# Places of activations in a line of 128 bytes, a block inverse in halves, and masks kept once

## The chip, the core and the metric

The kernel runs on one core of a Trainium2 chip. The core has a matmul engine (PE, whose weight loads are listed apart as PEld), three elementwise engines (DVE, ACT, POOL) and queues that start transfers (SP, ACT, POOL). A tile lies in the on-chip memory as 128 partitions with a line of bytes in each; matmuls write to PSUM, a second memory. The metric is device time in microseconds (us) of one execution; lower is better.

## What is computed

A small network on one sequence of 256 positions of width 1024: one block of four linear-attention mixers, cross-attention to a memory of 256 rows and a convolutional feed-forward layer; then two blocks of attention (three kinds of heads) and feed-forward. Cut to what the change touches, the second mixer solves a triangular system for each head and each chunk, here of 128 positions:

```python
kk    = where(strict, k @ k.T * ratio, 0)           # below the diagonal
a_mat = eye(c) + beta[:, None] * kk
u_v   = triangular_solve(a_mat, beta[:, None] * v, lower=True, unit_diagonal=True)
w_k   = triangular_solve(a_mat, (beta * gamma)[:, None] * k, lower=True, unit_diagonal=True)
```

Everything else that the change touches is products of float32 matrices: activations (256 positions) times weights.

## The kernel before, in words

Every large product is made from halves of the numbers: an activation or a weight `a` is kept as an upper part `hi` (float32r) and a rest `lo = a - hi`, and a product is three matmuls, hi by hi, lo by hi, hi by lo (`mm_f`, L429, L430, L431). In `mm_f` the weights are the stationary operand (128 columns), the activations the moving one (256 columns). `mm_t` (L440 to L442) has them the other way round. Weights arrive in chunks of 512 KB on SP's queue; ACT makes `whi` (L410) and DVE `wlo` (L411).

The activations' tiles are `xh` and `xl` (input of a stage, eight blocks of 256 columns), `oh`/`ol`, `xoh`/`xol`, `aoh`/`aol` (input of an output product), `gh`/`gl` (the feed-forward layer's inner width, 22 blocks) and `mh`/`ml` (the memory). One block is 1024 bytes in a partition, so all blocks of a tile begin at the same place in a line of 128 bytes; which place that is follows from what is allocated ahead of it. All weight blocks of 128 columns begin at place 0. `GPAD` (L50) is a tile of some columns ahead of `gh`, and moves it.

Stages follow one another: the mixers (`block1_mix`, to some 245 us), cross-attention (to 323), feed-forward f0 (`psU` is its upward product, `psD` its downward one, to 510), attention 0 (to 648), feed-forward l0f (to 832), attention 1, feed-forward l1f.

The triangular solve stands in `delta` (L852). It works on eight matrices of 128x128 (two chunks t, four heads h) in `An`, and builds the inverse by doubling the block size: at level k, blocks of b = 2^k are joined. `TT` is the inverse transposed, `Tm` the inverse. A level multiplies `An` with the left columns of `Tm` (`psy`, L980), masks (`Y`, DVE, L982), multiplies with `TT` (`psu`, L994) and adds to `Tm` (DVE, L995); then `Tm` is transposed on PE (`psw`, L1002) and copied to `TT` (ACT, L1003). There are six levels; the sixth adds to `TT` alone (L990). Each `yield` hands over to the next of three generators: `weave` (L778) runs `delta`, `hgrn` and `turns` in turn, and a scheduler orders the instructions of each engine from that.

The masks `triu` and `strict` lie in the tile `cst1`, and are copied by DVE to `levr` (L912, L913), whose first 896 columns come by a transfer from POOL's queue (L750).

Of the kernel before, what the change touches and what calls it, by code (L numbers as in the profile page):

```python
# [8 lines left out]
F32 = mybir.dt.float32  # L9
F32R = mybir.dt.float32r  # L10
# [6 lines left out]
P = 128  # L17
# [32 lines left out]
GPAD = {"f0": 8, "l0f": 16, "l1f": 72}  # L50
# [145 lines left out]
def const_arrays():  # L196
# [16 lines left out]
    c1["triu"] = (i[:, None] <= i[None, :])  # L213
    c1["strict"] = (i[:, None] > i[None, :])
# [20 lines left out]
    c1["mk"] = np.concatenate(mk[1:], 1)  # L235
    c1["decay"] = dec.reshape(P, -1)
    c1["lev"] = np.concatenate(lev, 1)
# [128 lines left out]
class Net:  # L366
# [27 lines left out]


# [143 lines left out]
    def xsplit(self, x, g, acts=None):  # L539
        xh, xl = acts or (self.act.tile([P, KD, T], F32R, tag="xh", name="xh"), self.act.tile([P, KD, T], F32R, tag="xl", name="xl"))  # L540
# [80 lines left out]
    def ffn(self, tag, g, fc, nt):  # L621
        nc = self.nc
        x = self.x
        xh, xl = self.xsplit(x, g)
        acc, = self.sumsq(x)
        with self.pool("ffn" + tag) as big, self.pool("fz" + tag, 3) as zp:
            big.tile([P, GPAD[tag]], F32, name="gpad")
            gh = big.tile([P, NFF, T], F32R, name="gh")
            gl = big.tile([P, NFF, T], F32R, name="gl")
# [72 lines left out]
    def block1_mix(self, es):  # L702
# [5 lines left out]
        n1 = _C1O["triu"][0]  # L708
# [6 lines left out]
        xh, xl = self.xsplit(x, self.par("mix"))  # L715
# [136 lines left out]
    def delta(self, s, sm, gates):  # L852
# [57 lines left out]
        tri, strict = self.c1("triu"), self.c1("strict")  # L910
# [46 lines left out]

        TM = b8.tile([P, 2, 2, 4, P], F32, tag="b8", name="TM")
        TT, Tm = TM[:, 0], TM[:, 1]
        idb = self.ident.unsqueeze(1).to_broadcast([P, 4, P])  # L960
        mi = lambda a: a.bitcast(I32)
        for t in range(2):
            nc.gpsimd.tensor_copy(TT[:, t], idb)
            odd = lambda a: a.rearrange("p h (n d) -> p h n d", d=2)[:, :, :, 1]
            nc.vector.copy_predicated(odd(TT[:, t]), mi(self.c1("mlev")[:, 0:64]).unsqueeze(1).to_broadcast([P, 4, 64]), odd(An[:, t]))
            pt = self.pb(512, "pstt")
            for h in range(4):
                self.tr(pt[:, h * P:(h + 1) * P], TT[:, t, h, :])
            nc.scalar.copy(fl(Tm[:, t]), pt)
        for k in range(1, 7):  # L970

            b = 1 << k
            mk = self.c1("mk")[:, (k - 1) * 64:k * 64].unsqueeze(1).to_broadcast([P, 4, 64])
            left = lambda a: a.rearrange("p h (n c d) -> p h n c d", c=2, d=b)[:, :, :, 0, :]
            yield
            Ys = []
            for t in range(2):
                py = self.pb(T, "psy")
                for h in range(4):
                    self.mm(py[:, h * 64:(h + 1) * 64].rearrange("p (n d) -> p n d", d=b), An[:, t, h, :], left(Tm[:, t])[:, h])  # L980
                Y = m.tile([P, 4, 64], F32, tag="Yl", name="Y", bufs=2)
                nc.vector.tensor_mul(Y, py.rearrange("p (h c) -> p h c", h=4), mk)  # L982
                Ys.append(Y)
            for t in range(2):
                Y = Ys[t]
                if k == 6:
                    pu = self.pb(512, "psu2")
                    for h in range(4):
                        self.mm(pu[0:64, h * P:(h + 1) * P], Y[:, h, :], TT[:, t, h, :])
                    nc.vector.tensor_add(fl(TT[0:64, t]), fl(TT[0:64, t]), pu[0:64])  # L990
                    continue
                pu = self.pb(T, "psu2")
                for h in range(4):
                    self.mm(pu[:, h * 64:(h + 1) * 64], TT[:, t, h, :], Y[:, h, :])  # L994
                nc.vector.tensor_add(left(Tm[:, t]), left(Tm[:, t]), pu.rearrange("p (h n d) -> p h n d", h=4, d=b))  # L995
            if k == 6:
                continue
            yield
            for t in range(2):
                pw = self.pb(512, "psw2")  # L1000
                for h in range(4):
                    self.tr(pw[:, h * P:(h + 1) * P], Tm[:, t, h, :])  # L1002
                nc.scalar.copy(fl(TT[:, t]), pw)  # L1003
# [276 lines left out]
    def keys_norm(self, mem):  # L1280
        nc = self.nc
        nc.sync.dma_start(mem, self.ap["memT"])
        self.mh = self.memp.tile([P, KD, T], F32R, name="mh")
        self.ml = self.memp.tile([P, KD, T], F32R, name="ml")
# [21 lines left out]
    def xattn(self, es):  # L1306
# [5 lines left out]
        xh, xl = self.xsplit(self.x, self.par("xat"))  # L1312
# [13 lines left out]
        oh = m.tile([P, KD, T], F32R, name="xoh")  # L1326
        ol = m.tile([P, KD, T], F32R, name="xol")
# [56 lines left out]
    def block2(self):  # L1384
# [5 lines left out]
        for l in range(2):  # L1390
            with ExitStack() as es:
                xh, xl = self.xsplit(x, self.par("ga1") if l else gg)
                self.attn(es, l, xh, xl)
# [6 lines left out]
        y = self.act.tile([P, KD, T], F32, tag="xh", name="y")  # L1400
# [23 lines left out]
    def attn(self, es, l, xh, xl):  # L1424
# [40 lines left out]
        self.mm_f(kk[0:96], a + "kk", range(KD), xh, xl)  # L1465
        lh = m.tile([P, 3, T], F32R, name="lath")
# [54 lines left out]
        oh = m.tile([P, KD, T], F32R, name="aoh")  # L1521
        ol = m.tile([P, KD, T], F32R, name="aol")
# [163 lines left out]
```

## Time and profile before

| | us |
|---|---|
| median of 3 runs | 1165.92 (1165.40 to 1167.05) |
| the profiled execution | 1163.74 |
| its span, first to last instruction | 1162.0 |
| PE busy | 1135.8 (98%) |
| DVE busy | 937.0 (81%) |
| ACT busy | 668.2 (58%) |

A matmul's record ends later than the next one's begins, so "busy" says that PE has work, not that it runs at its best. What a matmul costs in a row of them is the distance from start to start: the length of a stretch plus one duration, divided by the count of records that touch the stretch.

### The profile page before, as it was taken

To read this page: it belongs to the slowest core of one execution; us is meant where nothing else is said; L and a number is where in the kernel's file an instruction comes from. 1 tells how busy PE (TensorE), PEld (TensorE's weight loads), DVE (VectorE), ACT (ScalarE), POOL (GpSimd) and SP (SyncE) were. 2 spreads that over 40 slices of the span, in tenths; PEclk is the share of its full clock that TensorE was granted. 3 is DMA by queue.
4 is the path that set the end of the run, shared out by engine and by line. 5 is a ranking of instruction groups with operands and counts; after the bars stand their busy time and mean duration, and the time that the engine had idled before them with its cause. 6 is when DMAs were issued, how large, how long until landed. Compare 5 with 4: busy or idle time off the path is not lost.

```text
span 1162.0 us, 23197 instructions
## 1 busy us (share of the span) xinstructions
PE 1135.8 (98%) x9148; PEld 1093.9 (94%) x9148; DVE 937.0 (81%) x1887; ACT 668.2 (58%) x1178; POOL 109.9 (9%) x137
## 2 busy tenths in 40 slices
PE   7999999999999999999999999999999999999996
PEld 7899888989999999998989999999998999999996
DVE  7887869587589997559898899986588978999854
ACT  6652545565476666554555676665445557766642
POOL 5501201010010000222000200001120002000000
PEclk9899999999999999999999999999999999999998
DMA  6522242556446656554423565565553235555652
GB/s 246 171 73 79 69 143 76 171 176 220 133 153 199 199 187 195 183 179 134 137 94 110 181 185 196 183 190 194 185 162 125 92 128 182 183 193 187 187 194 85
DMA packets 51948, 184.68 MB, mean 159 GB/s; under 512 B 5888, under 2 KB 6784, under 8 KB 51584
## 3 DMA queue, kind: packets, MB, share of 16 engines
q1 hardware_dynamic: 51408, 182.23, 49.0%
q8 instruction: 71, 1.16, 0.4%
q10 hardware_dynamic: 288, 0.52, 0.1%
q0 software_dynamic: 144, 0.46, 0.1%
q14 instruction: 37, 0.30, 0.1%
HBM read 182.14 MB, written 1.05 MB: 158 GB/s over the span
## 4 chain that ended last, share of the span: by engine, by line
PE 89%; DVE 7%; ACT 2%; issue 1%; DMA 0%; SPq 0%; POOL 0%; DVEq 0%; ACTq 0%
PE psU L431 10%; PE psU L430 10%; PE psU L429 10%; PE psD L430 5%; PE psD L431 5%; PE psD L429 5%; PE psp L429 3%; PE po L451 3%; PE psp L430 3%; PE psp L431 3%; PE psW L429 3%; PE psW L431 3%; PE psW L430 2%; PE pst L442 2%; PE pst L440 2%; PE pst L441 2%
## 5 line engine op out<-in xcount | busy, mean ns | idle before, releaser
L410 ACT ACTIVATE whi<-raw 128x1024 fp32r<-128x1024 f32 (+5 forms) x411 | 362.9, 898 | 304.6 <-PE psU L430 53.7
L411 DVE TENSOR_TENSOR wlo<-raw,whi 128x1024 fp32r<-128x1024 f32 (+5 forms) x411 | 424.2, 1044 | 136.4 <-ACT whi L410 134.2
L429 PE MATMUL psU<-xh,whi 128*128 128x256 f32 x1056 | 295.4, 280 | 0.0
L431 PE MATMUL psU<-xh,wlo 128*128 128x256 f32 x1056 | 294.9, 279 | 0.2 <-DVE wlo L411 0.2
L430 PE MATMUL psU<-xl,whi 128*128 128x256 f32 x1056 | 294.8, 279 | 0.0
L431 PEld LDWEIGHTS psU<-xh,wlo 128*128 128x128 f32 x1056 | 198.5, 188 | 0.4 <-DVE wlo L411 0.4
L429 PEld LDWEIGHTS psU<-xh,whi 128*128 128x128 f32 x1056 | 198.5, 188 | 0.1
L430 PEld LDWEIGHTS psU<-xl,whi 128*128 128x128 f32 x1056 | 198.5, 188 | 0.1
L429 PE MATMUL psD<-gh,whi 128*128 128x256 f32 x528 | 146.8, 278 | 0.0
L430 PE MATMUL psD<-gl,whi 128*128 128x256 f32 x528 | 146.8, 278 | 0.0
L431 PE MATMUL psD<-gh,wlo 128*128 128x256 f32 x528 | 146.8, 278 | 0.0
L534 POOL TENSOR_TENSOR ssa<-ssa,ssq 128x256 f32<-128x256 f32 x61 | 56.5, 931 | 711.6 <-ACT ssq L532 440.7
L666 DVE SCALAR_TENSOR_TENSOR y<-zb,prm,y 128x256 f32<-128x256 f32 x264 | 113.9, 477 | 0.0
L430 PEld LDWEIGHTS psD<-gl,whi 128*128 128x128 f32 x528 | 99.2, 188 | 0.0
L431 PEld LDWEIGHTS psD<-gh,wlo 128*128 128x128 f32 x528 | 99.2, 188 | 0.0
L429 PEld LDWEIGHTS psD<-gh,whi 128*128 128x128 f32 x528 | 99.2, 188 | 0.0
L429 PE MATMUL psp<-xh,whi 128*128 128x256 f32 (+1 forms) x288 | 83.8, 291 | 0.0
L430 PE MATMUL psp<-xl,whi 128*128 128x256 f32 (+1 forms) x288 | 82.6, 287 | 0.0
L431 PE MATMUL psp<-xh,wlo 128*128 128x256 f32 (+1 forms) x288 | 82.4, 286 | 0.0
L657 ACT ACTIVATE y<-zb,prm 128x256 f32<-128x256 f32 x132 | 67.2, 558 | 6.6 <-DVE zb L653 6.6
L440 PE MATMUL pst<-whi,xh 128*128 128x256 f32 (+3 forms) x176 | 56.9, 324 | 0.0
L429 PEld LDWEIGHTS psp<-xh,whi 128*128 128x128 f32 (+1 forms) x288 | 54.2, 188 | 2.4 <-issue 2.3
(456 smaller groups left out, 2337.6 us busy)
## 6 DMA issues: line engine op xcount, KB each, us to landing
raw<-in_wst_dram SPq DMA_DIRECT2D x319, 512.0 KB, 3.5
raw<-in_wst_dram SPq DMA_DIRECT2D x5, 448.0 KB, 3.3
cst<-in_c_dram SPq DMA_DIRECT2D x1, 1664.0 KB, 7.4
raw<-in_wst_dram SPq DMA_DIRECT2D x3, 396.0 KB, 3.1
mem<-in_memT_dram SPq DMA_DIRECT2D x1, 1024.0 KB, 5.0
raw<-in_wst_dram SPq DMA_DIRECT2D x2, 480.0 KB, 4.1
raw<-in_wst_dram SPq DMA_DIRECT2D x2, 420.0 KB, 6.8
raw<-in_wst_dram SPq DMA_DIRECT2D x2, 384.0 KB, 4.0
```

What stands on the lines that cost most here:

```text
L410: nc.scalar.activation(hi[:, a:b], raw[:, a:b], AF.Copy)
L411: nc.vector.tensor_sub(lo[:, a:b], raw[:, a:b], hi[:, a:b].bitcast(F32))
L429: nc.tensor.matmul(ps, wh, xh[:, k, :], start=s, stop=False, skip_group_check=True)
L430: nc.tensor.matmul(ps, wh, xl[:, k, :], start=False, stop=False, skip_group_check=True)
L431: nc.tensor.matmul(ps, wl, xh[:, k, :], start=False, stop=e, skip_group_check=True)
L440: nc.tensor.matmul(pss[t], xh[:, k, a], wh, start=i == 0, stop=False, skip_group_check=True)
L441: nc.tensor.matmul(pss[t], xl[:, k, a], wh, start=False, stop=False, skip_group_check=True)
L442: nc.tensor.matmul(pss[t], xh[:, k, a], wl, start=False, stop=i == n - 1, skip_group_check=True)
L451: self.nc.tensor.matmul(out, lhsT, rhs, start=start, stop=stop, skip_group_check=True)
L534: (eng or nc.gpsimd).tensor_add(acc, acc, sq)
L657: nc.scalar.activation(y[:, e, u, :], z[:, e, 2:], AF.Identity, scale=fc[:, c + 2:c + 3], **kw)
L666: nc.vector.scalar_tensor_tensor(y[:, e, u, :], zs[u][:, e, j:j + T], fc[:, c + j:c + j + 1], y[:, e, u, :], ALU.mult, ALU.add)
```

## The change

Three things are changed.

First, the upper part and the rest of an activation are put into one tile (`duo`), each at a place in the line that a table `LINE` sets, another pair for each stage; `PAD` keeps the start of the tile fixed. The places that follow from the allocations of the two programs, in bytes (upper part, rest), with the number of triples of `mm_f`:

| product | triples | before | after |
|---|---|---|---|
| mixers, feature-major (psz, psq, psr) | 90 | 32, 32 | 64, 32 |
| keys of the memory (psk) | 64 | 96, 96 | 96, 0 |
| mixers' output (psW of oh) | 64 | 96, 96 | 64, 64 |
| cross-attention queries (psq) | 64 | 32, 32 | 32, 64 |
| cross-attention output (psW of xoh) | 64 | 0, 0 | 0, 96 |
| f0 up (psU) | 352 | 32, 32 | 64, 0 |
| f0 down (psD) | 176 | 32, 32 | 96, 64 |
| attention 0 (psp) | 143 | 32, 32 | 64, 96 |
| its output (psW of aoh) | 64 | 0, 0 | 96, 96 |
| l0f up (psU) | 352 | 32, 32 | 0, 64 |
| l0f down (psD) | 176 | 64, 64 | 0, 32 |
| attention 1 (psp) | 143 | 32, 32 | 32, 0 |
| its output (psW of aoh) | 64 | 0, 0 | 48, 112 |
| l1f up (psU) | 352 | 32, 32 | 32, 96 |
| l1f down (psD) | 176 | 32, 32 | 96, 32 |

Second, the block inverse works on sixteen matrices of 64x64, two to each of the eight: rows 0 to 63 and rows 64 to 127 side by side in the partitions. There are five levels on them, and a last one that joins the two halves. A matmul has 64 rows and 64 stationary columns; the two of a pair lie in opposite corners of PE's array. The turn is a matmul with the identity instead of a transpose.

Third, `triu` and `strict` come with the transfer of `levr`, which grows from 896 to 1152 columns; DVE's two copies go, and what read the masks in `cst1` reads them in `levr`.

```diff
-GPAD = {"f0": 8, "l0f": 16, "l1f": 72}
+PAD = {"m": 24, "xo": 24, "lat": 16, "g": 16}
+LINE = {"mix": (64, 32), "xat": (32, 64), "f0": (64, 0), "l0": (64, 96), "l0f": (0, 64), "l1": (32, 0), "l1f": (32, 96),
+        "f0g": (96, 64), "l0fg": (0, 32), "l1fg": (96, 32), "mh": (96, 0), "oh": (64, 64), "xoh": (0, 96), "aoh0": (96, 96), "aoh1": (48, 112)}
...
+    def duo(self, pool, n, key, base, name, **kw):
+        both = pool.tile([P, 2 * n * T + 64], F32R, name=name, **kw)
+        out = []
+        for i, r in enumerate(LINE[key]):
+            a = i * (n * T + 32) + (r - base) % 128 // 4
+            out.append(both[:, a:a + n * T].rearrange("p (k t) -> p k t", k=n))
+        return out
...
-                nc.gpsimd.dma_start(self.levr[:, 0:896], self.ap["c1"][:, _C1O["lev"][0]:])
+                nc.gpsimd.dma_start(self.levr, self.ap["c1"][:, _C1O["lev"][0]:])
...
-        nc.vector.tensor_copy(lev[:, 896:1024], tri)
-        nc.vector.tensor_copy(lev[:, 1024:1152], strict)
+        tri, strict = lev[:, 896:1024].bitcast(F32), lev[:, 1024:1152].bitcast(F32)
...
+        def turn(dst, src):
+            pw = self.pb(512, "psw2").rearrange("p (g c) -> p g c", g=8)
+            for g in range(8):
+                for r in halves:
+                    self.mm(pw[r, g, :], src[r, g, :], self.ident[r, r])
+            nc.scalar.copy(dst, pw)
...
-        for k in range(1, 7):
+        turn(Tm, Tx)
+        for k in range(1, 6):
...
+            py = self.pb(T, "psy").rearrange("p (g n d) -> p g n d", g=8, d=b)
+            for g in range(8):
+                for r in halves:
+                    self.mm(py[r, g], An[r, g // 4, g % 4, r], left(Tm)[r, g])
+            Y = m.tile([P, 8, 32], F32, tag="Yl", name="Y")
+            nc.vector.tensor_mul(Y, py.rearrange("p g n d -> p g (n d)"),
+                                 self.c1("mko")[:, (k - 1) * 32:k * 32].unsqueeze(1).to_broadcast([P, 8, 32]))
+            pu = self.pb(T, "psu2").rearrange("p (g c) -> p g c", g=8)
+            for g in range(8):
+                for r in halves:
+                    self.mm(pu[r, g, :], Tx[r, g, :], Y[r, g, :])
+            nc.vector.tensor_add(left(Tm), left(Tm), pu.rearrange("p g (n d) -> p g n d", d=b))
...
+            turn(Tx, Tm)
...
+        for g in range(8):
+            self.mm(py[up, g, :], An[lo, g // 4, g % 4, up], Tm[lo, g, :])
+        Y = m.tile([P, 8, 64], F32, tag="Yl", name="Y")
+        nc.scalar.copy(Y[up], py[up])
+        for r in halves:
+            nc.gpsimd.tensor_copy(g8(TT)[r, :, r], Tx[r])
...
+        for g in range(8):
+            self.mm(pu[lo, g, :], Y[up, g, :], Tx[up, g, :])
+        nc.vector.tensor_copy(g8(TT)[lo, :, up], pu[lo])
```

The first level on PE, before (`psy`, `psu`, `psw` are the inverse's; `psq` is the product of `hgrn` that stands between them):

```order
L451 MATMUL psy<-TM,An 128x64 x8
L429 MATMUL psq<-xh,whi 128x256
L430 MATMUL psq<-xl,whi 128x256
L431 MATMUL psq<-xh,wlo 128x256
L429 MATMUL psq<-xh,whi 128x256
L451 MATMUL psu_866<-Y,TM 128x64 x4
L451 MATMUL psu_872<-Y,TM 128x64 x4
L430 MATMUL psq<-xl,whi 128x256
L455 MATMUL psw_894<-ident,TM 128x128 x4
```

The same place on PE after:

```order
L469 MATMUL psy<-TM,An 64x32 x16
L447 MATMUL psq<-xh,whi 128x256
L448 MATMUL psq<-xh,whi 128x256
L449 MATMUL psq<-xh,wlo 128x256
...
L469 MATMUL psu_876<-Y,TM 64x32 x16
L449 MATMUL psq<-xh,wlo 128x256
...
L469 MATMUL psw_910<-ident,TM 64x64 x16
L448 MATMUL psq<-xh,whi 128x256
```

Twice as many matmuls stand in a block, each with half the rows and half the columns; eight matmuls of `psq` lie between the first two blocks instead of four, and the turn is one block of sixteen. (Since both parts now lie in one tile, the names read `xh` for `xl` too.) On DVE, around the second level, before (`Y` masks, line 995 adds; `wlo` is the weights' rest, the others are work of `hgrn` and of the chunks):

```order
L1149 TENSOR_TENSOR qbD<-psq,iy 64x2x128
L982 TENSOR_TENSOR Y<-psy,cst_141 128x256 x2
L411 TENSOR_TENSOR wlo<-raw,whi 128x512
L1190 TENSOR_TENSOR f<-f,l 128x512
L995 TENSOR_TENSOR TM<-TM,psu_964 128x64x4
L995 TENSOR_TENSOR TM<-TM,psu_970 128x64x4
L411 TENSOR_TENSOR wlo<-raw,whi 128x512
```

And after:

```order
L1173 TENSOR_TENSOR qbD<-psq,iy 64x2x128
L1214 TENSOR_TENSOR f<-f,l 128x512
L1004 TENSOR_TENSOR Y<-psy,cst_141 128x256
L429 TENSOR_TENSOR wlo<-raw,whi 128x512 x2
L1010 TENSOR_TENSOR TM<-TM,psu_991 128x64x4
L1173 TENSOR_TENSOR qbD<-psq,iy 64x2x128 x2
```

One mask and one addition stand where there were two of each, at the same place among the other work.

Behind the mixers the two programs issue the same instructions in the same order on every engine; only addresses differ.

## Rows read from the trace of the kernel before

**Rows 1.** The page: busy time, share of the span, instructions.
```profile
span 1162.0 us, 23197 instructions
...
PE 1135.8 (98%) x9148; PEld 1093.9 (94%) x9148; DVE 937.0 (81%) x1887; ACT 668.2 (58%) x1178; POOL 109.9 (9%) x137
```

**Rows 2.** Busy time by stretch; columns: stretch, length, engines (records), PE clock, DMA.
```profile
63.90:124.40 60.50, 59.55 (x482) 56.67 (x482) 45.88 (x110) 27.61 (x54) 2.92 (x4) 1.00 0.23 79
...
323.00:448.00 125.00, 124.80 (x1065) 124.34 (x1064) 118.20 (x183) 80.72 (x120) 5.20 (x11) 1.00 0.59 187
```

**Rows 3.** The same view, of instructions on tile psD alone: f0, then l0f.
```profile
450.00:500.00 50.00, 50.00 (x431) 50.00 (x430) 2.51 (x6) 1.00 0.61 188
...
775.00:825.00 50.00, 50.00 (x444) 50.00 (x443) 2.41 (x6) 1.00 0.60 196
```

**Rows 4.** The same of tile psk (mh), then psW (oh, then xoh).
```profile
207.00:216.00 9.00, 9.00 (x77) 9.00 (x76) 0.00 (x0) 1.08 (x3) 1.00 0.53 173
...
222.00:238.00 16.00, 16.00 (x135) 15.93 (x134) 1.38 (x4) 1.00 0.53 171
...
305.00:319.00 14.00, 14.00 (x120) 14.00 (x119) 0.15 (x1) 1.00 0.56 161
```

**Rows 5.** Groups by line, 63.8 to 124.5 us: busy, mean ns, idle before.
```profile
L451 PE MATMUL psy<-TM,An 128*128 128x64 f32 x96 | 11.6, 273 | 0.0
...
L451 PE MATMUL psu<-Y,TM 128*128 128x64 f32 x80 | 9.8, 273 | 0.9 <-DVE Y L982 0.9
...
L451 PEld LDWEIGHTS psu<-Y,TM 128*128 128x128 f32 x80 | 9.4, 191 | 1.5 <-DVE Y L982 1.5
...
L455 PE MATMUL psw<-ident,TM 128*128 128x128 f32 x40 | 5.3, 272 | 0.0
...
L982 DVE TENSOR_TENSOR Y<-psy,cst 128x256 f32<-128x256 f32 x12 | 4.8, 418 | 2.2 <-PE psy L451 2.0
...
L995 DVE TENSOR_TENSOR TM<-TM,psu 128x256 f32<-128x256 f32 x10 | 4.2, 421 | 4.2 <-PE psu L451 4.2
...
L451 PEld LDWEIGHTS psu<-TM,Y 128*64 128x64 f32 x16 | 1.7, 137 | 0.2 <-issue 0.2
...
L990 DVE TENSOR_TENSOR TM<-TM,psu 64x512 f32<-64x512 f32 x2 | 1.4, 680 | 1.1 <-PE psu L451 1.1
```

**Rows 6.** The chain that ended last, 63 to 125 us: start, us, what.
```profile
66.36 1.73 PE psy L451 x16
...
70.52 0.44 PE psw L455 x4
...
92.33 0.61 ACT Ehalf L1064
...
103.09 2.00 PE psu L451 x16
...
106.11 1.08 issue
...
111.54 2.00 PE psu L451 x16
```

**Rows 7.** That chain by line, from the head of the same answer.
```profile
by line: PE psu L451 20.6%; PE psy L451 11.3%; PE psc L451 7.0%; PE psl L451 6.5%; issue 5.3%; DVE wlo L411 4.9%; PE psw L455 4.2%; DVE R L1125 4.1%; PE psq L431 3.1%; PE psq L429 3.1%; PE psq L430 3.1%; DVE Pm L1136 3.0%; PE psr L429 2.3%;
```

**Rows 8.** PE in order of time: start, us, what, at three places.
```profile
67.90 0.36 PE L429 MATMUL psq<-xh,whi 128*128 128x256 f32 x1
68.10 0.28 PE L430 MATMUL psq<-xl,whi 128*128 128x256 f32 x1
...
152.51 0.92 PE L451 MATMUL psr<-rotrq,rotrk 64*128 64x256 f32 x4
...
579.77 0.93 PE L451 MATMUL pss<-rk,rq 64*128 64x128 f32 x8
```

**Rows 9.** Tile levr: its transfer and its readers; then line 923.
```profile
L750 POOL DMA_DIRECT2D levr<-in_c_dram x1: 772/772/772, 38.5 to 38.5; - x1
...
DMA to landing us min/median/max: 4.9/4.9/4.9
...
L923 DVE TENSOR_TENSOR G<-cst,ghi x2: 680/680/681, 51.2 to 51.8; 128x512 fp32r<-128x512 f32 x2
```

More of the change, by code (lines that the diff above doesn't have):

```diff
@@ L234, in const_arrays @@
     c1["mlev"] = np.concatenate(mt, 1)
-    c1["mk"] = np.concatenate(mk[1:], 1)
+    own = lambda a: np.where(i[:, None] < 64, a[:, :a.shape[1] // 2], a[:, a.shape[1] // 2:])
+    c1["mko"] = np.concatenate([own(a) for a in mk[1:6]], 1)
+    c1["m0o"] = own(mt[0])
+    c1["ido"] = own(np.eye(P))
     c1["decay"] = dec.reshape(P, -1)
-    c1["lev"] = np.concatenate(lev, 1)
+    c1["lev"] = np.concatenate(lev + [i[:, None] <= i[None, :], i[:, None] > i[None, :]], 1)
     c2["ident"] = np.eye(P)
@@ L393, in pool, with pad @@
         return self.tc.tile_pool(name=name, bufs=bufs, **kw)
+    def duo(self, pool, n, key, base, name, **kw):
[5 more added lines that the diff above has]
+        return out
+    def pad(self, pool, key):
+        pool.tile([P, PAD[key]], F32, name="pad" + key)
     def load(self, upto):
@@ L537, in sumsq, with xsplit @@
         return [[a] + last[i:i + 1] for i, a in enumerate(accs)]
-    def xsplit(self, x, g, acts=None):
-        xh, xl = acts or (self.act.tile([P, KD, T], F32R, tag="xh", name="xh"), self.act.tile([P, KD, T], F32R, tag="xl", name="xl"))
+    def xsplit(self, x, g, key):
+        xh, xl = self.duo(self.act, KD, key, 32, "xh", tag="xh")
         for k in range(KD):
@@ L958, in delta @@
         TM = b8.tile([P, 2, 2, 4, P], F32, tag="b8", name="TM")
[L959 to L969, printed above, removed]
@@ L970, in delta @@
-        for k in range(1, 7):
+        TT = TM[:, 0]
+        Tm, Tx = (TM[:, 1, i].rearrange("p h (u c) -> p (h u) c", u=2) for i in range(2))
+        halves = [slice(0, 64), slice(64, P)]
+        nc.gpsimd.memset(TT[64:P, :, :, 0:64], 0.0)
+        nc.gpsimd.tensor_copy(Tx, self.c1("ido").unsqueeze(1).to_broadcast([P, 8, 64]))
+        odd = lambda a: a.rearrange("p g (n d) -> p g n d", d=2)[:, :, :, 1]
+        m0 = self.c1("m0o").bitcast(I32)
+        for r in halves:
+            for t in range(2):
+                nc.vector.copy_predicated(odd(Tx[r, 4 * t:4 * t + 4]), m0[r].unsqueeze(1).to_broadcast([64, 4, 32]), odd(An[r, t, :, r]))
@@ L975, in delta @@
             yield
[L976 to L995, printed above, removed]
@@ new lines, in delta @@
+            yield
+            turn(Tx, Tm)
+        yield
+        lo, up = halves
+        g8 = lambda a: a.rearrange("p t h c -> p (t h) c")
+        py = self.pb(512, "psy").rearrange("p (g c) -> p g c", g=8)
+        for g in range(8):
+            self.mm(py[up, g, :], An[lo, g // 4, g % 4, up], Tm[lo, g, :])
+        Y = m.tile([P, 8, 64], F32, tag="Yl", name="Y")
+        nc.scalar.copy(Y[up], py[up])
+        for r in halves:
+            nc.gpsimd.tensor_copy(g8(TT)[r, :, r], Tx[r])
+        pu = self.pb(512, "psu2").rearrange("p (g c) -> p g c", g=8)
@@ L1282, in keys_norm @@
         nc.sync.dma_start(mem, self.ap["memT"])
-        self.mh = self.memp.tile([P, KD, T], F32R, name="mh")
-        self.ml = self.memp.tile([P, KD, T], F32R, name="ml")
+        self.pad(self.memp, "m")
+        self.mh, self.ml = self.duo(self.memp, KD, "mh", 64, "mh")
         g = self.par("memw")
@@ L1325, in xattn @@
         nc.vector.tensor_scalar(sc, rT, 1.0 / 16.0, None, ALU.mult)
-        oh = m.tile([P, KD, T], F32R, name="xoh")
-        ol = m.tile([P, KD, T], F32R, name="xol")
+        self.pad(m, "xo")
+        oh, ol = self.duo(m, KD, "xoh", 64, "xoh")
         def scores(h):
@@ L1399, in block2 @@
         rB = self.inv_root(self.st, *self.mean(self.sumsq(x, join=False, eng=nc.vector)[0], "irv"), "nB")
-        y = self.act.tile([P, KD, T], F32, tag="xh", name="y")
+        y = self.act.tile([P, 2 * KD * T + 64], F32, tag="xh", name="y")[:, 0:KD * T].rearrange("p (k t) -> p k t", k=KD)
         for k in range(KD):
@@ L1520, in attn @@
         vL = m.tile([P, 2, 512], F32, name="vL")
-        oh = m.tile([P, KD, T], F32R, name="aoh")
-        ol = m.tile([P, KD, T], F32R, name="aol")
+        oh, ol = self.duo(m, KD, f"aoh{l}", 64, "aoh")
         sel = m.tile([P, 384], F32, name="sel")
```

29 lines of the change are left out of this document (9 added, 20 removed).

## Prediction, made before the changed kernel ran

> **What bounds the kernel now.** I read the page's busy line first: PE has work in 98% of the span, DVE in 81%, ACT in 58% [rows 1]. So what PE does from one matmul to the next is the time, and the question is whether a stretch is limited by PE's own pace or by a feeder. The stretches answer that. Within the downward products PE is never idle and DVE has little to do with the tile [rows 3]. In the upward product of f0 PE is idle for 0.2 of 125 us, but DVE is busy for 118.2 of them [rows 2], so there PE and DVE are near each other. In the stretch of the inverse PE is busy 59.55 of 60.5 us and DVE 45.88 [rows 2], but the busy share hides that single blocks wait for one another: there the chain of waits counts, and I read it last.
>
> PE's own pace is not one number. The downward products of f0 and l0f issue the same matmuls at the same granted clock, 1.00 (the 2.4 GHz level). In 50 us one has 431 records, the other 444 [rows 3]. With one duration of 0.28 us added to the stretch, a matmul costs 50.28/431 = 116.7 ns in f0 and 50.28/444 = 113.2 ns in l0f. The one thing that sets them apart in the table of places is that gh and gl begin at place 32 in f0 and at 64 in l0f. Three short products give the other places [rows 4]: psk at 96 takes 9.28/77 = 120.5 ns, the mixers' output at 96 takes 16.28/135 = 120.6, the output of cross-attention at 0 takes 14.28/120 = 119.0. Three are from short stretches, good to about 1 ns; the order 64, 32, 0, 96 I take as it is. In all of these the upper part and the rest share one place, so no row shows a mixed pair.
>
> **The change, part by part.**
>
> **Places.** A triple of mm_f reads the upper part twice and the rest once, so it costs 2p(h) + p(l) if each matmul goes by the place of what it reads itself. p is 119.0 at place 0, 116.7 at 32, 113.2 at 64 and 120.5 at 96. Places 48 and 112 occur in no row; I put them midway between their neighbours (115 and 119.8), and bound them by 113.2 and 120.6. The feed-forward products, in order: f0 up goes from 350.1 ns a triple to 345.4, times 352 is -1.65 us; f0 down from 350.1 to 354.2, times 176, +0.72; l0f up to 351.2, +0.39; l0f down from 339.6 to 354.7, +2.66, the largest term, since this product leaves the best pair; l1f up to 353.9, +1.34; l1f down to 357.7, +1.34. That is +4.8. The rest: mixers' feature-major products -0.63, psk -0.10, mixers' output (from 361.5 to 339.6, times 64) -1.40, queries and output of cross-attention -0.22 and +0.10, attention 0 with its output -0.46 and +0.29, attention 1 with its output +0.33 and -0.46. That is -2.55, and the whole **+2.2 us**. Gains in f0 up may be partly lost, since DVE there has only 6.8 us to spare [rows 2]; losses count in full, because PE is the later one in each of these stretches. The bounds: if every matmul ran at 113.2 the sum would be -25.6, at 120.5 it would be +25.8. Products whose activations are the stationary operand (mm_t) have no row that tells a place of weights alone; I put them at nothing, and the places' spread of 113.2 to 120.6 over their 240 records bounds them by about 1.8 us either way.
>
> The Trainium skill, "TensorE: Matmul & The Clock Gate", section "Part 2: What happens when you issue a matmul", says that the engine reads from two independent ports, so that loading the next tile's weights takes nothing from the read bandwidth of the running matmul. By it alone places would be no term, and the sum would be the inverse's alone. The trace speaks against resting on that: weights always begin at place 0 here and the pace still moves by 7 ns with the activation's place.
>
> **The inverse on PE.** Before: six levels of 16 + 16 records at 128 columns or fewer, 192 in all, and 48 transposes. A block of 16 records stands 1.73 us on the chain, 108 ns a record; four transposes take 0.44 us [rows 6]. So it is 192 x 0.108 + 48 x 0.110 = 26.0 us of PE. (The mean of 273 ns in the groups [rows 5] is the record's length, not its pitch.) What a record costs with 64 columns loaded no row shows directly. The weight load falls from 191 to 137 ns between 128 and 64 columns [rows 5], 54 ns less, and 108 - 54 gives an estimate of **55 ns**. After: 272 matmuls, two records each. 256 of them form pairs in opposite corners of the array. Do the two of a pair overlap? The nearest row: the eight records of a pair of heads (rk by rq), four on each of two row groups of 64, take 0.93 us, and the four records of one such head in the mixers, one after the other, 0.92 us [rows 8]; both sets have two records of 128 columns and two of 256 for a head, the row printing the first one's shape. Two row groups thus go through together. I take that: 256 pairs of records at 55 ns are 14.1 us, and 32 unpaired records 1.8. Each of 17 blocks also costs an entry: from a block's end to its next neighbour's start the first psq matmul takes 0.20 us instead of 0.117 [rows 8], so 17 x 0.085 = 1.4. Sum 17.3 against 26.0, **-8.7 us** on PE.
>
> How much of it is on the path? In 62 us of the chain, psu, psy and psw hold 20.6 + 11.3 + 4.2 = 36.1%, 22.4 us of those 26 [rows 7]. So 0.86 of it counts: **-7.5 us**. That needs DVE and ACT not to be later. The chain has stretches without PE, behind 92.33 and in the 1.08 us of issue at 106.11 [rows 6], where DVE and ACT set the end. The change takes work off DVE: twelve masks become five (7 x 0.418), ten additions five (5 x 0.421), the two of L990 (0.680 each) one copy [rows 5], near -5.8 us altogether. That is the cover under which PE's gain comes through; without it the gain is nothing. The copies of TT on POOL go beside the last psy and psu, POOL being busy 2.92 us of this stretch [rows 2].
>
> **Masks.** Two DVE copies ahead of the chunks go, some 0.4 us by the duration of a 256-column mask [rows 5], hidden. levr's transfer grows by 256/896 = 29%; it was issued at 38.5 and landed 4.9 us later, at 43.4. Even with 29% more it lands at some 44.8, and its first reader, G, starts at 51.2 [rows 9]: 6 us of slack, cost nothing. Were the cover gone, it would cost about 1.4 us. cst1's second transfer becomes shorter, nothing. Behind the mixers no instruction moves.
>
> **The sum.** -7.5 + 2.2 = -5.3 us on a profiled execution of 1163.74, so 1158.4. The median of the runs is 2.2 us above that execution; carried over, **1160.6 us**.
>
> **Rivals.**
>
> *B, the corners don't overlap (slower).* The heads of the row that shows overlap write two PSUM tiles [rows 8]; the two corners of the inverse write one PSUM tile, the upper half of the partitions and the lower. If that makes them wait for each other, all 544 records cost 55 ns in sequence: 29.9 + 1.4 - 26.0 = +5.3 us on PE, times 0.86 is +4.6; with the places +6.8: **1172.7**. It decides from the point at which a pair costs 89 ns and more for the inverse itself; with the places against it, from 79 ns. For it: no row has two tiles of the array writing one PSUM tile. Against it: the matmuls of a pair touch different partitions.
>
> The Trainium skill states a rule that speaks for B: "TensorEngine Tiling (Array Packing)", section "Restrictions and Gotchas", says that different row tiles cannot access the same PSUM bank at the same time. No run here shows it yet; by it the time would be B's.
>
> *C, the worse of a pair sets the pace.* If alternating between two places costs a re-alignment, a triple goes at three times the worse place: the sum of the table is then +17.9, with the inverse +10.4: **1176.3**. For it: places 32, 0 and 96 cost every matmul something over 64, and no row shows a cheap place staying cheap when the read ahead of it is a dear one. Against it: nothing in the rows has a pace above the dearest place.
>
> *D, mixing relieves.* If what costs is two reads in a row from the same place, a mixed pair goes by its better place: -12.7, with the inverse -20.2: **1145.7**. For it: f0 up and f0 down share place 32 and still differ, 125.28/1065 = 117.6 against 116.7 [rows 2, 3], so a place alone doesn't settle the pace. Against it: that difference is small, and DVE is close behind PE in f0 up.
>
> *E, the inverse's gain is swallowed.* If the chain through the inverse is held by DVE and ACT's other work (the chunks' R and Pm and the weights' rests stand in it with 4.1, 3.0 and 4.9% [rows 7]), PE's 8.7 us turn into waits, and the places alone stay: **1168.1**. For it: DVE is busy 76% of this stretch. Against it: DVE loses work as well.
>
> **How the numbers follow.** A has 0.47, B 0.13, C 0.13, D 0.15, E 0.12. A's own range, by the bounds of its inverse (nothing to -11, for records at 40 ns) and of the places by a third of their spread, is 1152 to 1168. To hold 8 in 10 the range takes in B and E and the near part of C and D: 1148 to 1175. About 0.2%, some 2.3 us, is what a measurement of this kernel can tell from no change. Faster by more: most of A and D, 0.57. Within: the edge of A and some of E, 0.13. Slower by more: B, C, and what is left of E, 0.30.
>
> **What would show it.** In the profile after, records on psD in 50 us: 50.28/0.1181 = 426 in f0 by A, 417 by C, 444 by D; in l0f 425 by A, 422 by C, 431 by D. A block of the inverse, 32 records, lasts some 0.9 us by A and 1.8 by B. The share of psu, psy and psw in the chain should fall from 36%, and if DVE's or ACT's rows grow in their place, E holds. G should still start behind other work and not behind levr's transfer. The prediction is wrong if the pace of a mixed pair lies outside its two places, if a block of the inverse takes over 1.2 us, or if the whole time falls on the other side of the one before.

## The result, and the profile after

The changed kernel takes 1174.59 us (1173.83 to 1175.20, three runs) against 1165.92 before: a ratio of 1.0074, 95% interval 1.0057 to 1.0091, so 8.7 us slower. Forecast were 1160.6 and "faster". The profiled execution took 1173.83, its span grew from 1162.0 to 1172.1 us.

The page after, to be laid beside [rows 1]:

```profile
span 1172.1 us, 23783 instructions
...
PE 1143.2 (98%) x9452; PEld 1098.1 (94%) x9452; DVE 934.0 (80%) x1874; ACT 666.0 (57%) x1173; POOL 111.3 (9%) x139
```

PE is busy for the same share: nothing new waits, PE itself is slower. Where, two stretches of the upward products tell. Columns as in [rows 2]: f0, then l0f, before:

```profile
325.00:445.00 120.00, 119.80 (x1023) 119.34 (x1022) 113.20 (x175) 77.61 (x115) 4.81 (x10) 1.00 0.60 189
650.00:770.00 120.00, 120.00 (x1029) 119.95 (x1028) 112.33 (x174) 80.14 (x113) 6.80 (x10) 1.00 0.59 189
```

and after:

```profile
325.00:445.00 120.00, 119.89 (x1007) 119.64 (x1007) 111.85 (x172) 75.68 (x110) 2.57 (x7) 1.00 0.56 186
650.00:770.00 120.00, 120.00 (x994) 119.95 (x993) 109.11 (x167) 77.61 (x110) 6.81 (x10) 1.00 0.56 184
```

With one duration of 0.28 us added to the stretch, a matmul in l0f went from 120.28/1029 = 116.9 to 120.28/994 = 121.0 ns, in f0 from 117.6 to 119.4; DVE did not become busier. The downward products, to be laid beside [rows 3], f0 (450 to 500 us) and l0f (780 to 830):

```profile
450.00:500.00 50.00, 50.00 (x425) 50.00 (x424) 2.50 (x6) 1.00 0.56 182
780.00:830.00 50.00, 50.00 (x421) 50.00 (x420) 2.44 (x6) 1.00 0.57 189
```

118.3 ns where 116.7 was, and 119.4 where 113.2 was. In what follows the pace of a product is the mean distance from the start of one of its matmuls to the start of the next, over the whole product, distances over 160 ns left out; it agrees with these quotients within half a nanosecond, but for f0 before. There the stretch holds the stage's start, with some gaps of 0.2 to 0.45 us from matmul to matmul; inside the product (tile psU) a matmul takes 100.28/860 = 116.6 ns:

```profile
340.00:440.00 100.00, 100.00 (x860) 100.00 (x859) 13.63 (x20) 1.00 0.60 190
```

So f0's upward and downward product, both at place 32, had the same pace, 116.7 ns, and the difference that the prediction read from [rows 2, 3] in favour of rival D was the start of the stage. Multiplied by the counts of matmuls, the change of pace over all products of `mm_f` gives +12.3 us: +4.4 for l0f's upward product, +3.1 for its downward one, +2.3 and +1.0 for f0's, +1.8 and +0.6 for l1f's, and -0.9 for the rest together.

The inverse did become cheaper. Chain of waits, 63 to 125 us: shares by line, then three of its pieces, beside [rows 6, 7]:

```profile
by line: PE psu L469 14.6%; issue 8.5%; PE psc L469 8.2%; PE psw L469 7.3%; PE psy L469 6.8%; PE psl L469 6.8%; PE psq L448 3.7%; DVE wlo L429 3.6%; PE psq L449 3.3%; PE psq L447 3.3%; DVE R L1149 3.1%; PE pst L460 2.9%; PE psr L448 2.6%; P
...
68.64 1.05 PE psy L469 x32
...
70.82 1.05 PE psu L469 x32
...
73.01 1.08 PE psw L469 x32
```

Its share fell from 36.1% to 28.7%, and "issue" rose from 5.3% to 8.5%. A block of 32 records takes 1.05 us, 33 ns a record. (psu is also the name of the solves behind the inverse; that holds before and after.) A block has edges, too. PE around one block, before and then in the first run below, which has the same inverse (start, us, what):

```profile
68.34 0.28 PE L429 MATMUL psq<-xh,whi 128*128 128x256 f32 x1
68.45 1.90 PE L451 MATMUL psu<-Y,TM 128*128 128x64 f32 x16
70.16 0.36 PE L430 MATMUL psq<-xl,whi 128*128 128x256 f32 x1
70.36 0.60 PE L455 MATMUL psw<-ident,TM 128*128 128x128 f32 x4
```

```profile
67.95 0.28 PE L448 MATMUL psq<-xh,wlo 128*128 128x256 f32 x1
68.16 1.12 PE L468 MATMUL psy<-TM,An 64*64 64x32 f32 x32
69.21 0.38 PE L446 MATMUL psq<-xh,whi 128*128 128x256 f32 x1
69.43 0.28 PE L447 MATMUL psq<-xh,whi 128*128 128x256 f32 x1
```

From the start of the psq ahead to the start of the second matmul behind it is 2.02 us before and 1.48 in the run; without two distances of 0.117, a block costs 1.79 and 1.25.

### The profile page after: what moved, and what is told of

Read it like the earlier page. It is cut to its first block, busy times and chain, and to the rows that moved or that the text cites. A ratio compares the mean times of both kernels' runs of the same rounds, so it can differ in the third digit from the quotient of the medians.

```text
span 1172.1 us, 23783 instructions
## 1 busy us (share of the span) xinstructions
PE 1143.2 (98%) x9452; PEld 1098.1 (94%) x9452; DVE 934.0 (80%) x1874; ACT 666.0 (57%) x1173; POOL 111.3 (9%) x139
## 3 DMA queue, kind: packets, MB, share of 16 engines
HBM read 182.07 MB, written 1.05 MB: 156 GB/s over the span
## 4 chain that ended last, share of the span: by engine, by line
PE 86%; DVE 9%; ACT 2%; issue 1%; DMA 0%; SPq 0%; POOL 0%; DVEq 0%; ACTq 0%
PE psU L448 11%; PE psU L449 11%; PE psU L447 10%; PE psD L449 5%; PE psD L447 5%; PE psD L448 5%; PE po L469 3%; PE psp L447 3%; PE psp L448 3%; PE psp L449 3%; PE psW L447 3%; PE psW L449 2%; PE psW L448 2%; DVE wlo L429 2%; PE pss L469 2%; PE pst L458 2%
## 5 line engine op out<-in xcount | busy, mean ns | idle before, releaser
L448 PE MATMUL psU<-xh,whi 128*128 128x256 f32 x1056 | 299.8, 284 | 0.0
L449 PE MATMUL psU<-xh,wlo 128*128 128x256 f32 x1056 | 297.9, 282 | 0.1
L447 PE MATMUL psU<-xh,whi 128*128 128x256 f32 x1056 | 295.8, 280 | 0.0
L447 PEld LDWEIGHTS psU<-xh,whi 128*128 128x128 f32 x1056 | 199.2, 189 | 0.1
L448 PEld LDWEIGHTS psU<-xh,whi 128*128 128x128 f32 x1056 | 198.8, 188 | 0.1
L447 PE MATMUL psD<-gh,whi 128*128 128x256 f32 x528 | 148.4, 281 | 0.0
L448 PE MATMUL psD<-gh,whi 128*128 128x256 f32 x528 | 148.4, 281 | 0.0
L448 PEld LDWEIGHTS psD<-gh,whi 128*128 128x128 f32 x528 | 99.3, 188 | 0.0
L447 PEld LDWEIGHTS psD<-gh,whi 128*128 128x128 f32 x528 | 99.2, 188 | 0.0
L447 PE MATMUL psp<-xh,whi 128*128 128x256 f32 (+1 forms) x288 | 83.7, 291 | 0.0
L448 PE MATMUL psp<-xh,whi 128*128 128x256 f32 (+1 forms) x288 | 82.8, 287 | 0.0
```

The lines of the kernel that those rows point to most:

```text
L447: nc.tensor.matmul(ps, wh, xh[:, k, :], start=s, stop=False, skip_group_check=True)
L448: nc.tensor.matmul(ps, wh, xl[:, k, :], start=False, stop=False, skip_group_check=True)
L449: nc.tensor.matmul(ps, wl, xh[:, k, :], start=False, stop=e, skip_group_check=True)
```

## Experiments

Places are given from here on in a line of 256 bytes, in which the weights begin at 128: the first 128 bytes hold the places 0 to 96, the second the same places as 128 to 224. Before, 32/32 was 160/160, l0f's 64/64 was 192/192, the two 96/96 were 224/224; of the products at 0/0, cross-attention's output was at 0/0 and those of the attentions at 128/128.

**The parts apart.** The first run keeps inverse and masks and puts every place back; the second keeps places and masks and takes the inverse of before (the second part of the change, undone word for word). The edit of the first:

```diff
-LINE = {"mix": (64, 32), "xat": (32, 64), "f0": (64, 0), ...
...
+LINE = {'mix': (160, 160), 'xat': (160, 160), 'f0': (160, 160), ...
...
-            a = i * (n * T + 32) + (r - base) % 128 // 4
+            a = i * (n * T + 64) + (r - base) % 256 // 4
```

> The changed kernel (block inverse in halves, masks in levr) with every activation back at the place it has in the kernel before, hi and lo alike, counted in a line of 256 bytes. Theory P (the places cost, the inverse gains little): summing the change of the mean distance from matmul to matmul over all mm_f products of the two traces gives +12.3 us for the places, and the span grew by 10.1, so the inverse is worth -2.2: about 1163.5. Rival Q (the inverse gains the forecast 7.5 and the places cost 16): about 1158.4. Rival R (the inverse itself loses): above 1166.

> The changed kernel with the inverse of the kernel before (eight matrices of 128x128); places and masks stay as changed. Theory P: 1174.6 + 2.2 = about 1176.8. Rival Q: about 1182. Rival R: below 1174.

The inverse alone: 1161.72 us against 1165.93 before in the same series, ratio 0.9972 (0.9957 to 0.9987); by the ratio that is -3.3 us with bounds of -5.0 and -1.5. The places alone: 1179.52, five runs from 1174.92 to 1181.03, ratio 1.0108 (1.0090 to 1.0127), +12.6 with bounds of +10.5 and +14.8. The sum, +9.3, is the changed kernel's +8.7 within these bounds. So the parts add up; the inverse gains 3.3 of the 7.5 forecast, 5.0 at most, and the places cost nearly six times the 2.2. Both times lie between those of theory P and of rival Q; rival R is out.

Where the inverse's gain went, the chain of the first run shows. Before, then the run:

```profile
56.66 1.86 PE psd L451 x8
...
116.67 1.78 PE psy L451 x16
...
121.91 0.89 PE psu L451 x8
...
123.56 0.84 PE psu L451 x8
```

```profile
57.49 1.87 PE psd L468 x8
...
64.91 0.68 PE psw L468 x16
...
66.49 0.61 PE psw L468 x14
...
68.23 1.05 PE psy L468 x32
...
114.03 1.07 PE psy L468 x16
...
118.83 0.89 PE psu L468 x8
```

From the first `psy` (66.36 before [rows 6]) to the end of the last it is 52.1 us before and 46.9 in the run: the levels gain **5.2**. But the first `psy` comes 1.9 later, and the first solve that uses the inverse (121.91 before, 118.83 in the run) 3.1 earlier. Of the 1.9, 0.8 stand ahead of `psd`: there the granted clock is at 1.2 GHz for some 3 us of the run, and was at 2.4 before; ahead of it, from 44 to 54 us, PE was busy throughout in both. Before, a like stretch lay at 28 to 36 us, where PE was idle in part (28 to 36 and 54 to 58 us, before and then the run):

```profile
28.00:36.00 8.00, 7.01 (x33) 6.81 (x34) 8.00 (x13) 4.23 (x10) 7.32 (x9) 0.57 0.45 110
54.00:58.00 4.00, 4.00 (x22) 3.10 (x21) 3.94 (x8) 1.01 (x3) 2.06 (x3) 1.00 0.47 158
```

```profile
28.00:36.00 8.00, 7.47 (x58) 7.16 (x57) 8.00 (x14) 5.17 (x13) 7.40 (x8) 1.00 0.50 152
54.00:58.00 4.00, 4.00 (x14) 3.30 (x15) 3.16 (x7) 0.17 (x2) 1.35 (x2) 0.59 0.41 141
```

The other 1.0 is the way in. The predicated copies that set up level 0 are twice as many, each of half the partitions and half the columns, and take 435 ns and not half of 722 (57 to 72 us, before and then the run):

```profile
L965 DVE COPY_PREDICATED TM<-cst,An 128x256 f32<-128x256 int32 x2 | 1.4, 722 | 0.0
```

```profile
L984 DVE COPY_PREDICATED TM<-cst,An 64x128 f32<-64x128 int32 x4 | 1.7, 435 | 0.0
```

The first turn waits for them in two pieces (64.91 and 66.49). The copies' own time explains only 0.3 of the 1.0 (1.7 against 1.4 us). The last copy also stands on DVE behind the second chunk's Pm, and the one turn needs both chunks, where before each chunk had four transposes of its own:

```profile
64.89 0.69 DVE L967 TENSOR_TENSOR Pm<-psg,E 128x512 f32<-128x512 f32 x1
...
65.93 0.45 DVE L984 COPY_PREDICATED TM<-cst,An 64x128 f32<-64x128 int32 x1
```

**The way in.** The products `Pm` are written behind these copies:

```diff
-        for dst, rhs in ((An, kb), (Pm, qh)):
+        def weigh(dst, rhs):
...
+        weigh(An, kb)
...
+        weigh(Pm, qh)
```

> The block inverse at the places of before (as the first run), with one edit: the weighting of the products of queries and keys (Pm, DVE) is written behind the inverse's predicated copies instead of ahead of them. If the inverse's late start is DVE's (the four copies of 64 partitions stand between Pm's four products, and the last ends at 66.3 us), the first block of the inverse comes 1 to 2 us earlier and the whole falls by as much, to about 1160. If PE or the two products ahead of it set that start, nothing moves: 1161.7.

1162.21 us, ratio 0.9982 (0.9972 to 0.9992): no gain over the first run. Its chain:

```profile
63.13 0.71 DVE TM L984 x2
...
63.86 0.73 DVE TM L984 x2
...
65.36 0.71 PE psg L468 x4
66.07 1.08 PE psw L468 x32
```

The copies end at 64.6 instead of some 66.4, but on PE four matmuls `psg` of `Pm` now stand ahead of the first turn and wait for a product of DVE, so the turn starts at 66.07 and `psy` at 68.16. The wait moved from DVE to PE's order. From the end of `psd` to `psy` it is 7.8 us before, 8.9 in the first run and 8.5 here (59.71 to 68.16), so some 0.4 of the 1.0 came back there, too little to show in the time. What the rest hangs on stays open.

**One place everywhere.** If place 192 cost 113.3 ns in itself, it should do so in every product.

```diff
+LINE = {'mix': (192, 192), 'xat': (192, 192), 'f0': (192, 192), ...
```

> The changed kernel with hi and lo of every stage at byte 192 of a line of 256, the place that gh and gl of l0f have in the kernel before, where a matmul took 113.3 ns. Theory P256 (the place of what is read, counted in 256 bytes from the same start as the weights at 128, sets the pace in every product): 113.3 ns everywhere, 25 us less than at the places of before, and with the inverse about 1138 to 1140. Rival S (113 belongs to the downward product of l0f, or the upward products are held by DVE, which is busy 118 of their 125 us): only products without DVE behind them gain, some 1150 or more.

1167.97 us, ratio 1.0024 (1.0013 to 1.0034). Neither theory held: the long products, with and without DVE behind them, take 117.6 to 117.8 ns alike. Downward product of f0:

```profile
450.00:500.00 50.00, 50.00 (x427) 50.00 (x426) 2.51 (x6) 1.00 0.59 189
```

l0f's downward product, untouched in weights, counts and place, takes 117.8 instead of 113.3. In the attentions and in the queries of cross-attention, stretches of 113.3 and of 117.8 stand side by side, and other matmuls on PE lie between them.

**A survey of same places.** The edit, for the feed-forward layers:

```diff
+LINE = {... 'f0': (0, 0), 'f0g': (32, 32), ... 'l0f': (64, 64), 'l0fg': (96, 96), ... 'l1f': (128, 128), 'l1fg': (224, 224), ...
```

> The changed kernel with hi and lo at one and the same place in each stage, another in each: f0 up 0, f0 down 32, l0f up 64, l0f down 96, l1f up 128, l1f down 224 (bytes in a line of 256), keys of the memory and attention 0 at 192, mixers and their output 64, attention 1 at 96. Theory P128 (the line has 128 bytes, as the change takes it): 64 goes like 192, 113.3 ns; 0 like 128, 119 to 120; 32 like 160, 116.7; 96 like 224, 120. Theory P256: 64 differs from 192, near 117.7 (the changed kernel's mixers' output, both parts at 64, took 117.3), and 32 and 96 are free. By P128 about 1165, by P256 about 1173.

One execution, 1166.55 us. Pace by place: 0: 118.7; 32: 117.3; 64: 113.7 in l0f's upward product, 117.3 in the mixers' output; 96: 118.3; 128: 120.0; 192: 117.8 (psk); 224: 120.0. In neither reading is it right: 64 and 192 behave alike, as a line of 128 bytes would have it, but 0 and 128, 32 and 160 (116.7), 96 and 224 differ. And 64, like 192, has two paces. The mixers' output shows it between programs, too: with both parts at 64 it took 117.3 ns in the changed kernel and here, but 113.5 in the run with the places alone.

**Two rhythms.** So the next theory: at 64 and 192 two rhythms hold themselves up, and what lies ahead decides.

```diff
+LINE = {... 'f0': (160, 160), ... 'l0f': (64, 64), ... 'l1f': (160, 160), 'f0g': (192, 192), 'l0fg': (64, 64), 'l1fg': (192, 192), ...
```

> The changed kernel with hi and lo at one place in each stage: 160 (of a line of 256 bytes) for the upward products of f0 and l1f and 192 for their downward products, 64 for both products of l0f, 64 for the mixers, their output and the output of cross-attention, 160 for its queries, 192 for the rest. Theory L (at place 64 or 192 two rhythms hold themselves up, 113.3 and 117.8 ns; what runs just ahead decides which is taken, and from place 160 it is 113.3, as the kernel before shows in l0f): the downward products of f0 and l1f take 113.3 where the run with 192 everywhere took 117.8. The whole is 1152 to 1154 where l0f's upward product takes 113.3 too, about 1159 where it takes 117.8. Rival M (the place sets the pace by itself, and 192 costs 117.8 outside l0f): both downward products 117.8, the whole 1163 or more.

Median 1163.43 us, ratio 0.9995 (0.9974 to 1.0016): as a time nearest to rival M, with twelve runs from 1154.6 to 1171.2. Inside the one profile, downward products of f0 and l1f, both at 192, both entered from 160:

```profile
450.00:500.00 50.00, 50.00 (x444) 50.00 (x443) 2.93 (x7) 1.00 0.59 197
...
1095.00:1145.00 50.00, 50.00 (x427) 50.00 (x426) 2.51 (x6) 1.00 0.54 175
```

113.3 and 117.8: the same places, the same instructions, the same clock. So rival M is out as well. The upward product of l0f, at 64 in the survey and here, shows the same across two programs (tile psU, the survey and then this run):

```profile
660.00:760.00 100.00, 100.00 (x885) 100.00 (x884) 13.66 (x20) 1.00 0.60 193
```

```profile
660.00:760.00 100.00, 100.00 (x851) 100.00 (x850) 12.49 (x19) 1.00 0.56 188
```

100.28/885 = 113.3 and 100.28/851 = 117.8 ns. That there are two rhythms is shown, and that place 160 ahead always gives the quick one is refuted. That the spread of the runs comes from it is only likely.

**Passing from 160 to 192.** The first block of each activation (two of `gh`, `gl`) stands 32 bytes lower, so that each output passes once:

```diff
+        a = self.at + lo * T - (self.by if lo < self.n0 else 0)
```

> All at 192 as in the third run, but the first block of each activation (blocks 0 and 1 of gh and gl) 32 bytes lower, at 160, so that products that go through the blocks pass from 160 to 192 again and again. Theory L: each passage can start the 113.3 rhythm; if it does so as in l0f of the kernel before, the long products fall from 117.8 to about 114 and the whole by some 17 to 20 us, to about 1149. Rival (a change of place in the stream costs by itself, as in the mixed pairs at 117.5 to 121): 1168 or more.

1159.22 us, ratio 0.9957 (0.9944 to 0.9970). The downward product of l0f, six stretches inside its outputs 2 to 7:

```profile
779.00:785.00 6.00, 6.00 (x55) 6.00 (x54) 0.00 (x0) 1.00 0.62 185
787.00:793.00 6.00, 6.00 (x54) 6.00 (x53) 0.00 (x0) 1.00 0.56 196
794.00:800.00 6.00, 6.00 (x55) 6.00 (x55) 0.41 (x1) 1.00 0.57 184
802.00:808.00 6.00, 6.00 (x53) 6.00 (x53) 0.41 (x1) 1.00 0.61 203
```

The eight outputs take 118.0, 113.4, 117.9, 114.0, 117.9, 114.0, 117.9 and 114.0 ns: six matmuls at 160 turn the rhythm over, every time. Half of the stage is quick, and the time is half of the forecast gain below the run with 192 everywhere.

More blocks at 160, another number in each stage:

```diff
+KICK = {'mix': 2, 'xat': 2, 'f0': 2, 'l0': 3, 'l0f': 3, 'l1': 4, 'l1f': 4, 'f0g': 4, 'l0fg': 6, 'l1fg': 8}
```

> The run with passages from 160 to 192, with more blocks at 160: 2 blocks for the upward product of f0, 3 for l0f, 4 for l1f; 4, 6 and 8 blocks of gh and gl for the downward products. In the run before each passage turned the rhythm over (outputs of l0f's downward product took 113.4 to 114.0 and 117.9 ns in turn). Theory L: what a passage does depends on how many products stand at 160; a length that leads to 113.3 from either rhythm would show as every output at about 114, a length that keeps the rhythm as a row of outputs of one kind. If the passage always turns it over, all stages alternate as before, and the time stays near 1159.

1159.32 us in one execution. In the downward products, with 12 and 24 matmuls at 160, the outputs of f0 (near 114.1) and l1f (near 114.8) are alike; with 18 (l0f) they alternate as with 6. The rhythm of place 160 repeats every four matmuls (118, 120, 113, 116 ns), and 12 and 24 are multiples of four. I took that as "leads to the quick one".

So four blocks everywhere:

```diff
+KICK = {'mh': 4, 'mix': 4, 'xat': 4, 'f0': 4, 'l0': 4, 'l0f': 4, 'l1': 4, 'l1f': 4, 'f0g': 4, 'l0fg': 4, 'l1fg': 4}
```

> The block inverse with all activations at 192 and the first four blocks of every xh, xl, gh, gl, mh, ml at 160: twelve (of 24) or twelve (of 66) matmuls in a row at 160, a multiple of the four of that place's rhythm. Theory L: every passage leads to 113.3, so the downward products take 114.1 in all outputs and the upward ones 115.5, as those stages with four blocks did in the run before; against the kernel with the old places and the same inverse (1161.7) that is -1.3 us for each upward product, -1.4 for the downward ones of f0 and l1f and +0.4 for l0f's, some -0.5 for each attention and -0.9 for psk: about 1154, with runs close together. Rival (the phase is set by chance at each start of a stage): 1157 to 1160 with a spread of several us, as in the runs with alternating outputs.

1157.71 us against 1166.82 before in the same series, ratio 0.9921 (0.9904 to 0.9939), 9 us faster and the quickest version found. But the reason given is half wrong, and the time and its spread (1154.9 to 1159.7) are the rival's. Downward products of f0 and l1f:

```profile
450.00:500.00 50.00, 50.00 (x440) 50.00 (x440) 2.93 (x7) 1.00 0.60 195
```

```profile
1090.00:1140.00 50.00, 50.00 (x427) 50.00 (x427) 2.94 (x7) 1.00 0.52 170
```

All outputs of f0 and l0f take near 114.1, all of l1f 117.6, and l1f's upward product 117.2 against 115.8 and 115.7 of the others. So twelve matmuls (and 24) keep the rhythm that is there, and six (and 18) turn it over; which one a stage starts with isn't controlled.

**Weights moved.** The tables' activations at 192, their tiles kept there, and the weights moved from 128 to 192 by a pad of 64 bytes:

```diff
+            self.whi.tile([P, 16], F32, tag="padw", name="padw", bufs=1)
```

> All activations at 192 as in the third run, the weights moved by 64 bytes, from 128 to 192. If only the activations' own place counts: 117.8 with stretches of 113.3, as there, about 1168. If the distance to the weights' place counts: as with activations and weights both at 128, where l1f's upward product took 120.0: about 1178.

One execution, 1182.73 us; downward product of l1f:

```profile
1110.00:1160.00 50.00, 50.00 (x419) 50.00 (x418) 2.51 (x6) 1.00 0.56 181
```

120.0 ns in all six long products, as with activations and weights both at 128. The mixers' output is not in the table and moved along to 0, a distance of 64 as 192 has from 128, and took 117.8, where place 0 with the weights at 128 took 118.7. So at the two distances tested the distance between the two places counts, not the activation's own place.

**Pairs handed round.**

```diff
-LINE = {... "f0": (64, 0), ... "l0f": (0, 64), ... "l1f": (32, 96),
-        "f0g": (96, 64), "l0fg": (0, 32), "l1fg": (96, 32), ...
+LINE = {... 'f0': (0, 64), ... 'l0f': (160, 96), ... 'l1f': (192, 128), 'f0g': (0, 160), 'l0fg': (224, 160), 'l1fg': (224, 64), ...
```

The first table counts in 128 bytes; in 256 its pairs are (192, 128), (0, 64) and (160, 96) for the upward products of f0, l0f and l1f, and (224, 64), (0, 160) and (224, 160) for the downward ones.

> The changed kernel with its pairs of places handed round among the three feed-forward layers, counted in a line of 256 bytes: the pair (0, 64) of l0f's upward product goes to f0, f0's (192, 128) to l1f, l1f's (160, 96) to l0f; the downward pairs likewise, (0, 160) to f0, (224, 160) to l0f, (224, 64) to l1f. Theory (a mixed pair has a pace of its own, whatever the stage): f0 up 120.8 ns, l0f up 118.5, l1f up 118.9, f0 down 119.3, l0f down 117.8, l1f down 118.5, and the whole as the changed kernel, 1173 to 1176, since the counts are the same. Rival (the stage, with what DVE and the transfers do in it, sets the pace of a mixed pair): f0 up 118.9, l0f up 120.8, l1f up 118.5 as before.

One execution, 1174.10 us. Upward products of f0 and l0f, to be laid beside the rows of after:

```profile
325.00:445.00 120.00, 119.95 (x991) 119.69 (x990) 110.38 (x170) 73.93 (x107) 2.55 (x7) 1.00 0.58 183
650.00:770.00 120.00, 120.00 (x1011) 119.81 (x1010) 111.05 (x171) 80.36 (x116) 7.48 (x11) 1.00 0.58 184
```

Paces: 120.9, 118.5 and 118.9 up, 119.3, 117.8 and 118.5 down, each within 0.1 ns of the expectation. In the six long products a mixed pair carries its pace with it; DVE and the stage don't set it.

## Why the prediction was wrong

The direction is wrong. That the time lies inside the range by 0.4 us is luck: the range went up to 1175 to hold rivals. Rival C's 1176.3 comes nearest, and for the wrong reason. Of the 14.0 us between 1160.6 and 1174.59, some 10 are the places (+12.3 for +2.2) and some 4 the inverse (-3.3 for -7.5).

- **The step that failed** is "a triple costs 2p(h) + p(l) if each matmul goes by the place of what it reads itself". By triples divided by three, forecast and measured, in ns: f0 up 115.1 and 118.9, l0f up 117.1 and 120.8, l0f down 118.2 and 119.3, f0 down 118.1 and 118.5, l1f up 118.0 and 118.5, l1f down 119.2 and 117.8. The pace belongs to the pair, whatever the stage. It may lie above both places (l0f up: 120.8, with 119.0 and 113.2 in the table) or below both (psk: 117.7, with 120.5 and 119.0). f0 up and l0f up alone, 3.8 and 3.7 ns on 1056 matmuls each, are 8 of the 10 us by which the places were missed.
- **The table beneath it** was wrong in two ways. "113.2 at place 64" came from one product, in one of two rhythms; the place also has 117.8. And places were counted in 128 bytes, where the survey parts 0 from 128, 32 from 160 and 96 from 224 by 0.6 to 1.7 ns. With the survey's paces, 160 at 116.7 and both 64 and 192 at 117.8, the same rule gives +9.3 us for the six long products (an estimate), where the prediction had +4.8 and the traces have +13.2. So about half of what was missed there is the table's, and half the rule's. Which rhythm a product meets was not controlled: the mixers' output, forecast at 113.2 with -1.40 us, took 117.3 in the changed kernel, and 113.5 at the same places in the run with the places alone.
- **Rival C** (the worse of a pair sets the pace) fits f0 up (118.9 and 119.0) and nearly l0f down (119.3 and 119.0), but not psk (117.7 and 120.5), l1f down (117.8 and 120.5) or l0f up (120.8 and 119.0). The counts on psD that were to decide didn't: f0 has 425 (426 by A), l0f 421 (422 by C). **Rival D** (mixing relieves) fits none of the six.
- **The corners overlap**, as forecast: 32 records of a turn, 64x64 in two corners, take 1.08 us, and 16 records of the last psy, 64x64 in one corner, 1.07. So rival B is out. The rule quoted there from the Trainium skill, "TensorEngine Tiling (Array Packing)", section "Restrictions and Gotchas", doesn't hold for these two corners, which write different partitions of one PSUM tile.
- **The inverse's size** was too large in the sum. A block of psy or psu gains 1.79 - 1.25 = 0.54 us on PE, where the sum had 0.76 (1.73 before, without edges, and 0.97 after): 2.2 us less over ten such blocks (an estimate from the one shown). A turn takes 1.08, where the sum had 0.97 and the transposes took 0.88 (two of 0.44 [rows 6]). There are eighteen blocks; the sum had seventeen. "0.86 of it counts" was also read too high: the 22.4 us of psu, psy and psw hold 1.7 of solves (121.91 and 123.56), so the share is 0.80. The levels gained 5.2. What the sum left out is the way in: the predicated copies, their place in DVE's order and the first turn behind them were given no price. That is about 1.0 us, and the clock ahead of `psd` 0.8 more in that profile. Rival E (swallowed by DVE) holds at most for a part: "issue" grew.
- **Masks**: as forecast in cost. The transfer landed 6.4 us after its issue at 39.7 (first run), at 46.1, and G started at 50.6, not behind it.
- The other citation from the Trainium skill, "TensorE: Matmul & The Clock Gate", section "Part 2: What happens when you issue a matmul", was read as making places no term. That reading is contradicted: the long products took 113.3 to 120.9 ns by places and rhythm alone, and moving the weights by 64 bytes took them from 117.8 to 120.0. Whether loading weights takes read bandwidth from the running matmul, which the page denies, no run here shows.

## What to carry over

A pace read from one stretch is a state, and not a price, until a second stretch with the same addresses shows the same pace; here the forecast of every place stood on one or two stretches, and the quickest place's row happened to be in the quicker of two rhythms. Costs of operands that alternate don't add up from the costs of each alone: a mixed pair needs its own row, or a run. And when many small blocks replace few large ones, price the edges of a block and the set-up ahead of the first: halving partitions and columns of a predicated copy took it from 722 to 435 ns, so twice as many took 1.7 us instead of 1.4, and the one turn behind them waits for the last.

## What the runs showed of the hardware

- A matmul of 256 columns in a row of such has several steady rhythms at a granted clock of 1.00 (2.4 GHz): 116.7, 120.0 and, at two places, both 113.3 and 117.8 ns are seen for equal places (117.3, 118.3 and 118.7 at 32, 96 and 0), 117.8 to 120.9 for the mixed pairs of the long products. At 192 with weights at 128 both 113.3 and 117.8 hold for a whole product of 528 matmuls.
- Where the weights were moved, the pace followed the distance between the moving operand's place and theirs: 128 and 128 or 192 and 192 take 120.0; 0 with weights at 192 took 117.8, a pace of 192 with weights at 128. Two distances were tested.
- Six or eighteen matmuls at 160 ahead of those at 192 turn the rhythm over, twelve or 24 keep it. What sets it at a stage's start stays open, and so does the mechanism; no run here took a rhythm apart further.
- 32 records of 64x64 in two opposite corners of the array, writing one PSUM tile, take 1.08 us; 16 records of one corner 1.07.
